# Moving the eight late adaLN modulation blocks of a hybrid backbone step from the recurrence stage to the projection stage, with a newly searched instruction order

## The chip, the core and the metric

The kernel runs on one core of a Trainium2 chip. The metric is the device time of one execution in microseconds, median of the runs; before the change three runs gave 1770.6 us (1767.48 to 1778.25). In what follows PE is TensorE, DVE is VectorE, ACT is ScalarE, POOL is GpSimd and SP is SyncE, which here only issues DMAs.

## The reference

One layer of a diffusion backbone is applied to 1024 latent tokens and 128 context tokens of 1024 features. Everything is f32.

```python
mod  = silu(c) @ ada_w + ada_b                 # (1024) @ (1024, 6144), for c and for c_ctx
shift1, scale1, gate1, shift2, scale2, gate2 = split(mod, 6)
h = rmsnorm(x, norm_mix_w) * (1 + scale1) + shift1
u = h @ w_in                                   # 1024 -> 4320 features
o_a = hgrn2_mixer(u[:, :2560])                 # 4 heads x 128, gated linear recurrence, both directions
o_b = rwkv7_mixer(u[:, 2560:])                 # 8 heads x 64, delta-rule state, both directions
x = x + gate1 * (concat(o_a, o_b) @ w_out)
h = rmsnorm(x, norm_ffn_w) * (1 + scale2) + shift2
x = x + gate2 * ((gelu(conv(h @ w_gate) + b) * (h @ w_up)) @ w_down)
y = rmsnorm(x, final_norm_w)
```

`shift1` and `scale1` (the first 2048 of the 6144 columns of `mod`) are needed by the first projection. The other 4096 columns, `gate1`, `shift2`, `scale2` and `gate2`, are needed only after the mixers.

## The kernel before

The kernel is written as a list of recorded operations, and a table puts them in order. `plan` records each call of an engine; a run of matmuls written under `plan.together()` is one operation and stays in one piece. `SEQUENCE` gives the order of all operations in the program, `ENGINE_OF` says for operations that may run on one of several engines (copies on ACT or DVE, stores issued by POOL or SP) which one it is, and `PLACE_OF` says for each tile which of its tag's buffers it takes. All three tables are numbers found by a search outside the kernel. An engine executes its own operations strictly in the order of `SEQUENCE`; semaphores make it wait for what it reads and for buffers to come free. All loads go through SP in that same order.

The work falls into five stretches on PE:

1. The start: the tokens are normed and transposed, and `mod_columns` computes the first 2048 columns of the modulation.
2. The projections: `proj` (L1070 to L1072) multiplies 128 columns of `w_in` with all 1152 tokens as three matmuls of 384 columns for each of 8 pieces of the contraction (two fp32r halves of weight and activation, three products). Between them stand the features of the RWKV mixer (`features`) and `elim`, which inverts the 32x32 blocks of the chunk systems. `elim` runs four times for the four head pairs `p` and once for the context; its PE work is L1462 and L1464, in PSUM tiles of the tag `el`.
3. The chains: `chains(g)` for the two groups `g` steps 18 times through the chunks of the RWKV recurrence. A step is `load_step` and `load_values` (L1694, L1696, L1703), the score products (L1713), a transpose (L1727), then L1760, a copy (L1762), L1767, a copy (L1769), L1775 and the outputs L1784 and L1786. `hgrn_block` (L1567 to L1633) and `hgrn_out` (L1658 to L1673), the last quarter of the projections (576 of the 2304 matmuls) and the first output projections (`wo_tile`, L1955 to L1957) are mixed in.
4. The output projection, norm and modulation of the remaining tiles.
5. The FFN: gate and up (L2065), then down (L2229).

`ada_block(b)`, b = 0 to 7, computes 512 of the late 4096 columns of `mod`. The bias `ada_b` is loaded as 4 rows (L966) into the tile `adab`, and 4 matmuls with the small constant `one` (L970) put it into one PSUM tile of the tag `a`. Four loads (L973) bring 512 KB of `ada_w` each into `adaw2`, which has two buffers, one in the SBUF tile `top` and one in `fx`; after each load 8 matmuls of 128 columns (L977), four at a time on different 32-column groups of PE, are added to the same PSUM tile. So one PSUM tile is held from the bias to the last of the 36 matmuls. ACT copies it to `adam` (L978), POOL or SP stores what is needed as rows (L980, L983), PE transposes it (L985) and DVE copies two columns of 4 into `modc` (L988). The tag `a` has four PSUM banks, which the chains and `hgrn_block` use as well. The loop over the chains calls `ada_block` after every second chunk step, so all eight blocks lie in stretch 3.

Names such as `top`, `low` and `fx` are large SBUF tiles in which `Layout` and `plan.tag` place the small ones; in the profile's rows and in the order an operand carries the name of the large tile. `banks` is all of PSUM.

Of the kernel before, what the change touches and what calls it, by code (L numbers as in the profile page):

```python
# [20 lines left out]
P = 128  # L21
# [3 lines left out]
KT = 8  # L25
NPAIR = 4
# [2373 lines left out]
```

## Time and profile before

| | |
|---|---|
| median of 3 runs | 1770.6 us |
| the profiled execution | 1778.03 us, span 1776.3 us |
| mean granted TensorE clock | 0.991 |
| PE busy | 1711.1 us, 96% of the span |
| DVE, ACT, POOL busy | 1424.9, 949.4, 354.6 us |
| moved by DMA | 352.97 MB, mean 199 GB/s |

The profile describes one execution, whose own time lies 7.4 us above the median of the runs. Its page gives the busy time of each engine, the span in 40 slices, the chain of work that ended last and the costliest groups of instructions. The trace behind it answers three more kinds of question that are used below: the busy time of each engine in a stretch of the span, who waited for whom in such a stretch, and the instructions in order of time. In an answer in order of time the second column is how long an instruction (or several alike) took by the record, and in brackets stands how long the engine sat idle before it and for whom. Matmuls overlap, so that the price of a group of matmuls is read from the start of the group to the start of the next instruction, not from the second column. A matmul in plain f32 has two records, one in fp32r has one.

### The profile page before, as it was taken

What the parts mean: (1) busy time and instruction counts of PE and PEld (TensorE: products, weight loads), DVE (VectorE), ACT (ScalarE), POOL (GpSimd) and SP (SyncE); (2) the same over time, 40 slices, a digit from 0 to 9 for tenths busy, and PEclk for the clock granted to TensorE, in tenths of its full rate; (3) what the DMA queues carried; (4) which work ended last, traced back from release to release, by engine and by line L of the source; (5) the groups of instructions that cost most, each with busy time, mean ns of one, the idle gap of its engine ahead of it and who ended that gap; (6) DMA issues with size and microseconds to landing.
All of it is one profiled execution on the core that took longest, in us unless ns stands there. A gap on an engine that the chain in (4) does not pass through costs nothing.

```text
span 1776.3 us, 44618 instructions
## 1 busy us (share of the span) xinstructions
PE 1711.1 (96%) x17726; PEld 1544.9 (87%) x17726; DVE 1424.9 (80%) x2722; ACT 949.4 (53%) x1977; POOL 354.6 (20%) x546
## 2 busy tenths in 40 slices
PE   6999999999999989999999999999999999999998
PEld 4888888889988888887877889999999999888886
DVE  6548988988787878786767888898888888979765
ACT  6655766662266655564645664444444444665542
POOL 2003133153311011112210013323333322000000
PEclk8999999999999999999989999999999999999999
DMA  9326456486676678889987657877877777898683
GB/s 308 98 86 163 109 136 154 120 227 208 183 225 196 203 214 277 275 279 265 312 245 271 224 120 146 176 152 160 170 156 153 158 158 157 274 316 275 196 273 130
DMA packets 341838, 352.97 MB, mean 199 GB/s; under 512 B 69817, under 2 KB 264398, under 8 KB 341278
## 3 DMA queue, kind: packets, MB, share of 16 engines
q1 hardware_dynamic: 287518, 284.85, 52.9%
q0 software_dynamic: 54112, 65.27, 19.2%
q8 instruction: 139, 2.28, 0.5%
q14 instruction: 69, 0.57, 0.1%
HBM read 254.99 MB, written 118.10 MB: 210 GB/s over the span
## 4 chain that ended last, share of the span: by engine, by line
PE 73%; DVE 4%; DMA 4%; ACT 3%; issue 1%; POOL 1%; SPq 0%; DVEq 0%; ACTq 0%; POOLq 0%
PE banks L2065 27%; PE banks L2229 14%; PE banks L1070 4%; PE banks L1072 4%; PE banks L1071 4%; PE banks L1713 2%; PE banks L1955 1%; PE banks L1957 1%; PE banks L1956 1%; PE banks L1582 1%; PE banks L1784 1%; PE banks L1627 1%; PE banks L1760 1%; PE banks L1767 1%; PE banks L1786 1%
## 5 line engine op out<-in xcount | busy, mean ns | idle before, releaser
L1070 PE MATMUL banks<-hh,wh 128*128 128x384 f32 x768 | 278.2, 362 | 0.6 <-DVE fx L1250 0.6
L1072 PE MATMUL banks<-hh,wl 128*128 128x384 f32 x768 | 258.7, 337 | 0.0
L1071 PE MATMUL banks<-hl,wh 128*128 128x384 f32 x768 | 258.4, 336 | 0.0
L2153 DVE SCALAR_TENSOR_TENSOR low<-low,pf 128x1024 f32<-128x1024 f32 x176 | 225.7, 1282 | 10.6 <-ACT low L2147 8.0
L2065 PE MATMUL banks<-qm,wh 128*128 128x320 f32 x968 | 223.4, 310 | 0.2 <-ACT wh L2035 0.2
L2065 PE MATMUL banks<-hbm,wh 128*128 128x256 f32 x880 | 162.9, 282 | 1.5 <-ACT low L1935 1.5
L2065 PE MATMUL banks<-qm,wl 128*128 128x320 f32 x528 | 162.8, 308 | 0.2 <-DVE wl L2035 0.2
L2065 PEld LDWEIGHTS banks<-qm,wh 128*128 128x128 f32 x968 | 161.0, 189 | 0.6 <-ACT wh L2035 0.5
L1070 PEld LDWEIGHTS banks<-hh,wh 128*128 128x128 f32 x768 | 144.8, 188 | 15.7 <-issue 9.3
L1071 PEld LDWEIGHTS banks<-hl,wh 128*128 128x128 f32 x768 | 145.2, 189 | 2.7 <-issue 1.2
L1072 PEld LDWEIGHTS banks<-hh,wl 128*128 128x128 f32 x768 | 144.9, 189 | 0.0
L2065 PEld LDWEIGHTS banks<-hbm,wh 128*128 128x128 f32 x880 | 139.3, 190 | 1.8 <-ACT low L1935 1.7
L2065 PE MATMUL banks<-ham,wh 128*128 128x256 f32 (+1 forms) x616 | 131.7, 294 | 0.0
L2065 PE MATMUL banks<-hbm,wl 128*128 128x256 f32 x440 | 124.4, 283 | 0.0
L2102 ACT COPY fx<-banks 128x256 f32<-128x256 f32 (+1 forms) x132 | 52.0, 397 | 110.2 <-PE banks L2065 98.2
L2065 PEld LDWEIGHTS banks<-ham,wh 128*128 128x128 f32 x616 | 101.4, 190 | 0.3
L2065 PEld LDWEIGHTS banks<-qm,wl 128*128 128x128 f32 x528 | 99.1, 188 | 0.4 <-DVE wl L2035 0.4
L2035 ACT CAST wh<-low 128x512 fp32r<-128x512 f32 x82 | 50.5, 618 | 69.4 <-PE banks L2065 60.5
L2065 PEld LDWEIGHTS banks<-hbm,wl 128*128 128x128 f32 x440 | 84.0, 191 | 0.0
L2065 PE MATMUL banks<-ham,wl 128*128 128x256 f32 (+1 forms) x264 | 77.0, 292 | 0.0
L2035 DVE TENSOR_TENSOR wl<-low,wh 128x512 fp32r<-128x512 f32 x82 | 56.2, 689 | 22.8 <-ACT wh L2035 20.7
L2035 ACT CAST wh<-wr 128x512 fp32r<-128x512 f32 x72 | 44.6, 622 | 54.3 <-PE banks L2065 43.8
(586 smaller groups left out, 4368.2 us busy)
## 6 DMA issues: line engine op xcount, KB each, us to landing
wr<-in_w_in_dram SPq DMA_DIRECT2D x34, 512.0 KB
d_t<-in_ffn_w_down_dram POOLq DMA_DIRECT2D x60, 256.0 KB, 6.5
low<-d_a SPq DMA_DIRECT2D x54, 256.0 KB
low<-d_ak SPq DMA_DIRECT2D x64, 192.0 KB
low<-d_kb SPq DMA_DIRECT2D x36, 256.0 KB
d_a<-low POOLq DMA_DIRECT2D x16, 576.0 KB, 4.7
top<-in_ada_w_dram SPq DMA_DIRECT2D x17, 512.0 KB
low<-in_ada_w_dram SPq DMA_DIRECT2D x32, 256.0 KB
```

Source lines behind the costliest of these rows:

```text
L1070: mm(o, wh[:, kt, :], hh[:, kt, c], kt == 0, False)
L1071: mm(o, wh[:, kt, :], hl[:, kt, c], False, False)
L1072: mm(o, wl[:, kt, :], hh[:, kt, c], False, kt == KT - 1)
L1582: mm(pv[r, i, :], xs[:, t0:t0 + 32], view(qy, t0, [[2 * m, 16 // m], [B + m, 2], [1, m]]), True, True)
L1627: mm(ps[:, i * P:(i + 1) * P], kt[:, i * P:(i + 1) * P], val[:, i, :], True, True)
L1713: mm(pa[h][:, P * w:P * w + P], kb[hc[h], w, :], W[hc[h], A0[h] + 192 * w:A0[h] + 192 * w + P], True, True)
L1760: mm(R[hc[h], 64 * w:64 * w + 64], av(h, w, 0), X[h][:, 0, w], True, True)
L2035: split(*w, src)
L2065: pe.matmul(o, a[:, kt, :], b[:, kt, :], start=start and first, stop=last, skip_group_check=not start)
L2102: act.copy(keep[n], y[:, 0:w])
L2153: dve.scalar_tensor_tensor(av, shifted(dy, dx), tap(3 * dy + dx), av, MUL, ADD)
L2229: pe.matmul(o, x, y, start=fresh and f, stop=l, skip_group_check=not fresh)
```

## The change

`ada_block` is called twice after each of the four `elim` calls of stretch 2, and no longer in the loop over the chains. Its bias rows now go into the zeroed tile `adam` itself, and the constant `one` has 128 rows. The sum over the four loads is no longer kept in PSUM: each group of 8 matmuls has a PSUM tile of its own (tag `el`, half a bank, now freed as soon as it is read); the first is copied to `adam` by ACT and the other three are added to it by DVE. `adaw2` and `adam` get places of their own in the first layout of `top`, one buffer each, for which the tile `ttd` of `elim` moves into `asys` and `pm` into `etmp`. All three tables are new; the words that came with the change say that the search's model now has the fetching of instructions in blocks. Matmuls are as many as before on PE (12977 instructions both times), DVE gets 24 additions, POOL 8 memsets.

```diff
-    N0, N1, NX = 9584, 14336, 4096
+    N0, N1, NX = 9584, 14368, 4096
...
-        .add("ako", 1024).add("asys", 1024).add("tsys", 1024).add("etmp", 256).add("ttd", 1024) \
-        .add("tn", 1024)
+        .add("ako", 1024).add("asys", 1024).add("tsys", 1024).add("etmp", 256) \
+        .add("tn", 1024).add("adaw2", 1024).add("adam", 128)
...
-        .add("lnr", 1024).add("sm", 32, 2).add("adab", 128).add("adam", 128)
+        .add("lnr", 1024).add("sm", 32, 2)
...
-    plan.tag("adaw2", [(top, 8786), (fx, 1536)], 1024)
...
-    plan.tag("el", [(mp, 512 * 6 + 256 * b) for b in range(4)], 256)
+    plan.tag("el", [(mp, 512 * 6 + 256 * b) for b in range(4)], 256, True)
...
-    one = cst("one", [4, 4, 32])
-    dve.tensor_copy(one, view(ident[0:4, :], 0, [[1, 4], [0, 32]]))
+    one = cst("one", [P, 4, 32])
+    dve.tensor_copy(one, view(ident, 0, [[1, 4], [0, 32]]))
...
     def ada_block(b):
 
         c0 = 2048 + 512 * b
-        br = tl("adab", [4, P])
-        ld(br, I["ada_b"][0, c0:c0 + 512].rearrange("(a b) -> a b", b=P))
-        ps, mr = pbank("a"), tl("adam", [P, P])
-        with plan.together(mr):
-            for q in range(4):
-                mm(ps[32 * q:32 * q + 32, 0:P], one[:, q, :], br, True, False)
+        mr = tl("adam", [P, P])
+        pool.memset(mr, 0.0)
+        ld(mr[0:4, :], I["ada_b"][0, c0:c0 + 512].rearrange("(a b) -> a b", b=P))
         for k0 in range(0, KT, 2):
+            ps = pbank("el", 256)
             w = tl("adaw2", [P, 2, 512])
             ld(w, I["ada_w"][0, k0 * P:(k0 + 2) * P, c0:c0 + 512].rearrange("(a p) n -> p a n", p=P))
             with plan.together():
+                if k0 == 0:
+                    for q in range(4):
+                        mm(ps[32 * q:32 * q + 32, 0:P], one[:, q, :], mr, True, False)
                 for a in range(2):
                     for q in range(4):
-                        mm(ps[32 * q:32 * q + 32, 0:P], sT[:, k0 + a, :], w[:, a, P * q:P * q + P], False, k0 + a == KT - 1)
-        act.copy(mr, ps[:, 0:P])
+                        mm(ps[32 * q:32 * q + 32, 0:P], sT[:, k0 + a, :], w[:, a, P * q:P * q + P], k0 > 0 and a == 0, a == 1)
+            if k0 == 0:
+                act.copy(mr, ps[:, 0:P])
+            else:
+                dve.tensor_tensor(mr, mr, ps[:, 0:P], ADD)
...
-        pq = pbank("a")
+        pq = pbank("el", 256)
...
-        ttd, tn = tl("ttd", [P, 32, 32]), tl("tn", [P, 32, 32])
+        ttd, tn = tl("asys", [P, 32, 32]), tl("tn", [P, 32, 32])
...
-        pm = tl("asys", [P, 8, 32])
+        pm = tl("etmp", [P, 8, 32])
...
         elim(*sys_, 32, p, "el")
+        for b in range(2):
+            ada_block(2 * p + b)
...
-    ctx_ = tl("ttd", [P, NPAIR, 128])
+    ctx_ = tl("tn", [P, NPAIR, 128])
...
-        if n % 2 == 0 and n:
-            if n // 2 <= 8:
-                ada_block(n // 2 - 1)
```

Three places show how the new order differs. The changed kernel's line numbers are 3 to 6 higher: its L978 is the L977 of before, its L1074 to L1076 are the projections L1070 to L1072, and so on as named.

The first place is on PE at the beginning of the projections, where the LoRA gate's small product (L1305 before, L1309 now) stands between projections. Before:

```order
L1070 MATMUL banks<-hh,wh_134 128x384
L1071 MATMUL banks<-hl,wh_134 128x384
L1072 MATMUL banks<-hh,wl_135 128x384
L1305 MATMUL banks<-low 128x512 x2
L1070 MATMUL banks<-hh,wh_134 128x384
L1071 MATMUL banks<-hl,wh_134 128x384
```

And now, with the second group of 8 modulation matmuls (L978) among them:

```order
L1074 MATMUL banks<-hh,wh_134 128x384
L1075 MATMUL banks<-hl,wh_134 128x384
L1076 MATMUL banks<-hh,wl_136 128x384
L1309 MATMUL banks<-low 128x512 x2
L978 MATMUL banks<-top,sT 32x128 x8
L1309 MATMUL banks<-low 128x512
L1074 MATMUL banks<-hh,wh_134 128x384
```

All 32 groups of 8 have moved into this stretch in this manner, each by itself; 24 projection matmuls and three L1309 lie between this group and the next one.

The second place is on PE late in the chains, at one of the last steps. Before, the modulation matmuls of block 7 (L970, L977) stand between a chain's L1760 and its L1767, and behind that:

```order
L1713 MATMUL banks<-low 128x128 x8
L1760 MATMUL banks<-low 64x64 x8
L970 MATMUL banks<-top,one 32x128 x4
L977 MATMUL banks<-top,sT 32x128 x8
L1767 MATMUL banks<-low 64x64 x8
L977 MATMUL banks<-fx,sT 32x128 x8
L1760 MATMUL banks<-low 64x64 x8
L1775 MATMUL banks<-low 64x64 x8
```

Now, at about the same step (L1766 was L1760, L1719 was L1713, L1773 was L1767, and L1958 to L1960 is the output projection):

```order
L1766 MATMUL banks<-low 64x64 x8
L1719 MATMUL banks<-low 128x128 x8
L1773 MATMUL banks<-low 64x64 x8
L1958 MATMUL banks<-ham,wh_134 128x512
L1959 MATMUL banks<-ham,wh_134 128x512
L1960 MATMUL banks<-ham,wl_136 128x512
L1766 MATMUL banks<-low 64x64 x8
```

Between a chain's two products now stands the other chain's score product, and an output projection where the second modulation group was.

The third place is SP's queue. Before, late in the chains, it ran as follows (L1696 loads the chain's matrices, L973 is the modulation's load, L966 its bias):

```order
L966 DMA top<-in_ada_b_dram 4x128
L973 DMA top<-in_ada_w_dram 128x2x512
L1696 DMA low<-d_ak_80 64x768
L1861 DMA top<-d_vb 128x1024
L983 DMA d_g_68<-top 2x128
L1703 DMA low<-d_v_85 64x4x64
L1696 DMA low<-d_ak_80 64x768
```

These loads now stand early in the projections (L971 was L973, L967 was L966, L1272 loads a projection's weights):

```order
L1272 DMA wr<-in_w_in_dram 128x8x128
L967 DMA top<-in_ada_b_dram 4x128
L1311 DMA d_g<-low 128x512
L971 DMA top<-in_ada_w_dram 128x2x512
L1272 DMA wr<-in_w_in_dram 128x8x128
L971 DMA top<-in_ada_w_dram 128x2x512
L1363 DMA d_v_84<-top 128x3x128 x2
```

Of the 32 loads of the modulation blocks 30 now stand in SP's queue ahead of the first load of the chains, and the last two just behind it; on PE all 32 groups stand ahead of the first score product of the chains.

More of the change, by code (lines that the diff above doesn't have):

```diff
@@ L122 @@
 SEQUENCE = [int(i) for i in """
[301 rows of a table removed]
[302 rows of a table added]
 """.split()]
 ENGINE_OF = (
-    "VVVAVAVAAAAAAVAVVVAVAAAVGGGGGSGGGGGSSGSSGGGAVAVVVAAVVVVAVVAVAAAAVVAVVVAAVVVVVAVAGASASASASASASVSASVVAGAASVAVASGSSAAAASSGSAAASAASAAAASSSSVAVASGSSAAVSSGV"
-    "SGVAAAAVAGSSGSGGSAAVAVAAGSSSSGGGSSSAGAGAGAAAAVVAAGSSSSGSSGGGGSSGSSGSGGGGGAAASGVSAAAVSSGSVAAVGSGSAVAGGASAAVASSSGAVAASSSSAAVSSAASSVAAAVAVSGGSSSGSAAAAAAA"
-    "SSGSSGSSGSSAGAGASAAAAVAAAGSSSGGGSGSSSSSSGSSGSSGSSAAAGGVGAVAASSGGVAVASGGSAAASAASAAAVSGGSVAAASGSSVAVGSGAGSVAVAAAASSSSSSGSAAVAAAASGSSSSGSSGSSSSAAAAVAAASG"
-    "GGSGGGSGGGSSGGGSGSGSSGAAASAAGVVAASSSSVAAAGSSSVAASAASVAAASSSSVAAASGSSVAASGAAGSVVAAAAVGSGSGGGSVAVAAAAGGGGSSSSGGGVAAAAAAAGGGGSSGSGGGSGGGGSGGSGSSGAASAASAA"
-    "SAGASASASASAGGSGAASAVSVASAGAGASAGASASGSGAASAASAASVSASASVSVSASSSGAASAASAASGSGSSSSGSGSGVVAAAVVGSSGGGGSGSGGGSGGSGSSGGSGAAAAAAAAVAAVVAAAGGAAAAAAGAAASGAAAA"
-    "GAASAGAAAAGGASASSAAAAAVAAAAAAAAASSAAVASSAAAAAAAAAAAAGGAASSVAAAVAAAAAAAAAASSVAAASSAAAAAAAGAGAAAAAGAGASSAAAAAAAAAAAAAAASSAAAASSSSSSGAAAVGAAVAAAAGAAASGAA"
-    "AAAAAAAAAAAAASGAAAASSAAVAAAASAGAAVAGAASAGAAAAAAAAVAAAAAASGAVVASGAAAVGAAAAAAAGAAAGSAAAAAAAAAAAAVAASSAAAASSSGSSSAAAAAGASAGAAAVGGAGASAAAAAVAAAAAVAAASSAAV"
-    "ASGAVAAGGAAAAAAAGAASGVAAVAAAAAAAAAAASSAAAASSAAAVGGAGASAAAAGGASAGAAAAAAAAAVAAAAASSAAVASSSSSGSAAAAAGGAAAAAAVAGAAGSVAAAAAAAAAAAAAASSAAVASSAAVAGGAAGAGAGAG"
-    "GGGAAAAAAAGAVGVGASGSSAAAAAAVAAAAAAAASGAAVASSAAAVAAAAAVVAGAAASSAAAAAAAAAAAAAAASSAAAVGSGSGGGAAAAGGASASAAVVGGVSAGSSGSAAAAGGAAAAAVGGAASGAAAAAGASASAAAAGGAS"
-    "ASGGSGAAAAGGVAAAAVGGVASSVVAVASAGVAVAASAGAAAASSSSSSSSSSSSSSSVAAAAAVASAAVAVAVAGGGGSGGSSGGGSGGSSGGGGGGGGGGGGGGGGGGGGGGGGGGGGGSGGGGSSSSSSSSSSSSSSSSSSSSSSS")
@@ new lines @@
+    "VVVAVAVAAVAAAAAAVVAVVAAASSSSSSSSGGGGGSGGGSSVVAVAVVAAVVAAVVAAVAAVVAAVAAAAVAVAVVVASAGASAGASVSAGAGASVVVSGASVVVASSSSAVAASSGSVAASAASAAAVGGSSVAAVGSGGAAAGGGV"
+    "SGVVAAAVASSGSSGSSAVVAVAAGSSGSSGGGSSASASAGAAVAAVAASSGSGGGGSSGSSSGSSGSGSSSGGSAAASGAGVAAASSGGVAAVGSSGVAASGASVAAASGSGAAVASSSSVAVSGAASGVVVAVAAGSSSSGSSVVAAA"
+    "AASGGSSSSSSGSAGAGASAAAAAAAASGGSGGSSSSGSSSSSSSGSSGGSAAASAASAAVASSSGVVVASSGSVAASAAGVVAVSSGGVAAASSSSVAAGSAVSSAAVVVVASGGGSGSSAAAAAAASSSSSSGSGSSSSGAAAAAAAA"
+    "GGSSGGGGSGGGGSSGSSGSGSGSAAASGAGVAAASSSGAAAASSGGVAASAASVAAASSSSVAAASSSGVAAGSGASSVVVAAAASSSSGGGGVVAAAAAGGGSSGGGSGSAVAAAAAAGGGGGGSGSGSGGGSGGSSSGGSSGGGGGS"
@@ new lines @@
+    "GSAASAASVASVSVGASASASAGSSGAAGAVGAASASAGAGASASASGSGAVSAASVAGVGASASVSAGASGGGAASAAGAASSSSGSGSGSGGGVVAAAVAGSGGGGSSGGSSGGGGGGGGSSSSAAAVAAAAVAVAAAAVAGAAVAAA"
+    "AGAAGSAAAAGGASASAAVAGAVSASAAAAAAAAAAAAAAASSAAVASSAAAAAGAAAAAAGAVAGGAAAAVAAAAAAAAAASSAAAAGSAAAAGAVSASAAAAAGAGAGAAAAAAAVAAAAVAASSAAAASSSSSGSAAVAGGAAAAAV"
+    "GAAAGGAAAAAAAAAAAAAAASSAAAAGGAAAVAAAGASAAAVAGAGAGAAAAAAAAAAAAAAASSAAVAGSAAAAAAAAAAAAGGAAGSAAAAAAAAAAAAAAVSGAAAAGSGGSGGAVAAGGAGAGAVAAGAAGAGAAAAAAAAAAAA"
+    "AAASSAAAASGAAAAGGAAAAAAGGAASSVVAVAAAAAAAAAAVSSAAAASGAAAAAAAGASAAAAAGAGASAAAAAAAVAAAAAAASSAAVASSGGSSGAAAAAGGAAAAAAAAGAASGAAAAAAAAAAAAAAAGSAAAAGGAAVAGGA"
@@ new lines @@
+    "AAAGAGAGGSSAAAAGGGGAVGVGASSSSAVAAAAAAAAAVAAASGAVVASSAAAVAGAVAAAVGGAASSAAAAAAAAAAAAAAASGAAAASSGGGGSAAAAGGAGAGAAVVGGVGAGAAAAGGAAAAAAAGAAGSAAAAGAAGASAAAA"
+    "GAAGASAAAAGGAAAAAAAAAVSGVVAAASVSVAVAASASAAAASGSGSSSSSSSSSSSVAAAAAVVGAAVAVAVAGGSSSSGGSGSSSSGGSSSGGGGGGGGGGGGGGGGGSSSGSGGGGGSSGGGSSSGSGSSSSSSSSSSGGSSSSS")
+PLACE_OF = (
+    "301286021164205633477410031320132320102031030123423013111000102013012340100210523140211047614023411105074210303013243101001010101001110110010131101001"
+    "100000100111010010010111100100111000001111000010110011100001120010111101100001101110110201313223131311010101101111010110010110100110101001101101001010"
+    "111101100110100101000100111100001110011100000202011121002110101110111111010010110010110000001011101001011011000110001011110003001011110110001011101033"
+    "321021111333121110111000101100110001000011111000111001001001011111101001100000111102200022023120000011101001101110101010000010100110111000101010001000"
+    "101011001110101011100010110011111100111000000010010110011110011110001010001111100010110000011010110000111000011100001011001111101000100000001100100020"
+    "121301010121023100101013212111002030002313101101032100100002112101130032210030000211101332323213313312021100001001101120001113010003212111030201101101"
+    "010201101002211121021321330100011201100020001321110000301001101112310020010011010011311001103130102003010110121110231231010101000310311102322321121300"
+    "110102100023021001310010313001011310000101010102003000121011000310001311310002000101101121013131024270301a103559167d329f463b88e1ac2b0edcf1330201110021"
+    "110113110002000141200011310014121100011013310010300103101100012013010010001103101100210000103021019082314567a01210102310210013201323011232001002110310"
+    "103230120198364571010230102030010022311121130211020122301120203022110030020032310120001101103220011232200231031112122020010023212300131121320130032001"
+    "111301210001311222033111030010121002310103221122131001220133010122021301022210110332210021132102022113310211000201211202100133331102002101120202120330"
+    "111201030210122003301211100221201002330131111021102001120203300112223301130221101001110102323022020031100130231120123101022311011022023101133112101010"
+    "201022311000311123100130211121013110212300202101031021132322111001001123100200101202230133102131001010200213102231131021131002112012301013120211130020"
+    "020133132001121310102023100021233111032022131020201013321110210110020133301010122110121000201312023101030232120003110102321001021210020013201682015473"
+    "1400213o2i3k020l1m1p2m383w0c160a2j33290o1s1l3e2n0h0u1v29382b34021c103s2y4m5i2l0d1b3o2w051q3k2g0f1x340t2013390j2z1c3e0i1h2u101035432023013p07521r66413x"
+    "2a5w1n4v214232100561j1ms3t8b5230g0qi2uy3614251co0pdl3054736f2k2r1625x1140a0h3406e3wn19jv2516m2zu2sip430553t10qo62160k2ga17em4536n3fs1cuc2100g0xq248z21"
+    "401u0w3t2z0539112k371a0n335130542f3s1q042g3x0d1w302t0j213401233y1942251i315o0u3a274f282k3n041b6e0v132h2r0s143221403412")
```

17 lines of the change are left out of this document (removed), and 603 rows, old and new, of the table SEQUENCE.

## The prediction

> **What bounds the kernel now.** I read the page first: its totals and the rows of 40 slices.
>
> ```profile
> span 1776.3 us, 44618 instructions
> PE 1711.1 (96%) x17726; PEld 1544.9 (87%) x17726; DVE 1424.9 (80%) x2722; ACT 949.4 (53%) x1977; POOL 354.6 (20%) x546
> PE   6999999999999989999999999999999999999998
> DMA  9326456486676678889987657877877777898683
> ```
>
> PE is busy for 1711.1 of 1776.3 us. Whatever changes the time must either change PE's work or fill part of the remaining 65.2 us, so the next question is where they lie. The busy time by stage answers it. Its columns are stretch, length, busy time of PE, PEld, DVE, ACT and POOL, granted TensorE clock, DMA share and GB/s; the stretches are the start, the projections, the chains, the rest of the output projection, FFN up and FFN down.
>
> ```profile
> 0.00:50.00 50.00, 36.38 (x275) 25.43 (x275) 32.85 (x97) 35.45 (x73) 9.52 (x29) 0.90 0.94 303
> 50.00:484.00 434.00, 428.30 (x4440) 386.63 (x4434) 338.92 (x685) 246.12 (x494) 112.97 (x215) 1.00 0.55 148
> 484.00:950.00 466.00, 431.57 (x7824) 377.33 (x7822) 361.14 (x868) 262.04 (x613) 79.70 (x146) 0.98 0.82 248
> 950.00:1037.00 87.00, 84.34 (x466) 70.34 (x460) 72.78 (x135) 59.19 (x129) 5.72 (x5) 1.00 0.71 230
> 1037.00:1520.00 483.00, 482.70 (x3627) 482.63 (x3628) 421.06 (x614) 220.57 (x430) 143.47 (x148) 1.00 0.76 156
> 1520.00:1776.30 256.30, 247.76 (x1112) 202.59 (x1110) 198.12 (x326) 126.07 (x242) 3.25 (x4) 0.99 0.75 245
> 650.00:900.00 250.00, 233.42 (x4315) 205.61 (x4304) 195.76 (x476) 143.34 (x328) 45.83 (x83) 0.99 0.91 278
> ```
>
> PE idles 13.6 us in the start, 5.7 in the projections (1.3%), 34.4 in the chains (7.4%), 2.7 behind them, 0.3 in FFN up and 8.5 in FFN down, almost all of that at the very end. The FFN is full and keeps its matmuls, so its 739 us stay, and the change can act only up to 1037 us. The chains are the loose stretch, and also the one in which DMA is busiest: 0.82 of the engines' time, 0.91 between 650 and 900 us, against 0.55 in the projections. The change takes work and loads out of the loose stretch and puts them into the full one. For the chains I asked for what PE waited there (who waited, for what: us in total, times, longest).
>
> ```profile
> PE banks L1713 <- DMA low<-d_ak: 5.8, 4, 2.5
> PE banks L1767 <- ACT low L1762: 3.2, 3, 1.6
> PE banks L977 <- DMA fx<-in_ada_w_dram: 1.1, 2, 0.7
> PE banks L977 <- DMA top<-in_ada_w_dram: 1.1, 1, 1.1
> PE banks L1727 <- DMA low<-d_kb: 1.0, 1, 1.0
> PE banks L1713 <- DMA low<-d_akp: 0.7, 1, 0.7
> ```
>
> Loads account for 9.7 us, of which 2.2 are the modulation's own; the other 24.7 of the 34.4 us are short waits for ACT and DVE, of which the second row is the longest kind.
>
> **Part 1: PE work added to the projections.** Nothing of a modulation block leaves PE; 32 groups of 8 matmuls, 8 biases and 8 transposes change their place. What a group of 8 costs by itself is seen where one stands before a projection (start, duration, instruction; 16 records are 8 matmuls).
>
> ```profile
> 742.08 0.33 PE L1071 MATMUL banks<-hl,wh 128*128 128x384 f32 x1
> 742.25 0.34 PE L1072 MATMUL banks<-hh,wl 128*128 128x384 f32 x1
> 742.52 0.40 PE L1582 MATMUL banks<-top 128*32 128x32 f32 x24
> 742.73 0.62 PE L977 MATMUL banks<-top,sT 128*32 128x128 f32 x16
> 743.28 0.44 PE L1070 MATMUL banks<-hh,wh 128*128 128x384 f32 x1
> 743.56 0.34 PE L1071 MATMUL banks<-hl,wh 128*128 128x384 f32 x1
> 693.90 0.42 PE L970 MATMUL banks<-top,one 4*32 4x128 f32 x8
> 694.25 0.40 PE L1582 MATMUL banks<-top 128*32 128x32 f32 x24
> 745.41 0.27 PE L985 MATMUL banks<-c_ident,top 128*128 128x128 f32 x1
> 745.61 0.40 PE L1582 MATMUL banks<-top 128*32 128x32 f32 x24
> ```
>
> From 742.73 to 743.28 the group costs 0.55 us. The projection behind it takes 0.28 instead of the 0.17 between two projections, and the projection ahead of the small matmuls 0.27: another 0.10 on each side. A group alone between projections thus costs 0.75, one beside other small work 0.55. By the new order 15 of the places have projections on both sides, 15 on one side and 10 on none, so I take 0.65: 32 x 0.65 = 20.8. The biases take 0.35 (693.90 to 694.25), 8 of them 2.8; the transposes 0.20 (745.41 to 745.61), 8 of them 1.6. Together **+25.2 us**, between 22.0 (all at 0.55) and 28.4 (all at 0.75). The projections are 98.7% full on PE, so nothing hides it.
>
> The Trainium skill (TensorEngine Tiling (Array Packing), Key Properties) says that changing the tiling mode drains TensorE, which speaks against setting 32-column groups singly between full-width projections. By that rule alone the dearer end would hold for every group, 28.4 instead of 25.2. The trace agrees that there is such a price, with 0.10 us on each side.
>
> DVE gets 24 additions of 128x128 out of PSUM. Their form is not in the trace. The nearest rows are the smaller copy of 128x4 (L988) and the addition of 128x256 (L1793), median ns in the middle:
>
> ```profile
> L988 DVE COPY modc<-banks x16: 143/152/163, 668.4 to 937.4; 128x4 f32<-128x4 f32 x16
> L1793 DVE TENSOR_TENSOR low<-banks,low x16: 405/420/425, 514.6 to 934.2; 128x256 f32<-128x256 f32 x16
> ```
>
> Between 0.15 and 0.42, halfway 0.29, is 7 us in all; DVE has 434 - 338.9 = 95 us free there, and no projection waits for a sum. I take 0 on the path; without the cover it would be 7. The 8 memsets are POOL's, which is idle for three quarters of this stretch: also 0.
>
> **Part 2: PE work gone from the chains.** The instructions of the two lines, taken alone in the same stretch (L970, then L977):
>
> ```profile
> 484.00:950.00 466.00, 3.60 (x64) 1.27 (x64) 0.98 0.82 248
> 484.00:950.00 466.00, 19.57 (x512) 12.98 (x512) 0.98 0.82 248
> ```
>
> With 1.6 for the transposes this is 24.8 us of busy time, but it overlaps with its neighbours. From start to start, a group of 8 costs 0.55 alone and less when two follow each other, as they do in most places here: with 0.40 for those it would be 32 x 0.40 + 2.8 + 1.6 = 17.2 (0.40 is my estimate from the 0.55 above less most of the switching). I take the middle, 21, so **-21 us**, between -17.2 and -24.8. Parts 1 and 2 together are **+4.2 us**, from -2.8 to +11.2: cutting the sum into four separate groups makes PE's work a little dearer.
>
> **Part 3: loads.** 31 or 32 loads of 512 KB, 16 MB, leave a stretch that moves 248 GB/s x 466 us = 116 MB: 14% less. What this can give is read from a step near the end of the chains. First PE, with the wait in brackets, then what SP issued ahead of it:
>
> ```profile
> 908.94 1.28 PE L1713 MATMUL banks<-low 64*128 64x128 f32 x16 [2.48 <-DMA low<-d_ak]
> 910.15 1.12 PE L1760 MATMUL banks<-low 128*64 128x64 f32 x16
> 911.20 0.65 PE L970 MATMUL banks<-top,one 4*32 4x128 f32 x8
> 911.78 1.08 PE L977 MATMUL banks<-top,sT 128*32 128x128 f32 x16
> 912.79 1.12 PE L1767 MATMUL banks<-low 128*64 128x64 f32 x16
> ```
> ```profile
> 896.58 0.38 SPq L973 DMA_DIRECT2D top<-in_ada_w_dram  x1
> 898.04 0.45 SPq L1696 DMA_DIRECT2D low<-d_ak  x1
> 902.73 0.46 SPq L1696 DMA_DIRECT2D low<-d_ak  x1
> ```
>
> The chain's second matrix load was issued at 902.73 behind a modulation load of twice its size, and PE stood for 2.48 us at 908.94. With the loads gone the modulation's own 2.2 us go for certain, and of the other 7.5 I take 40%, 3: **-5.2 us**, between -2.2 and -9.7. What is late next in such a step is the copy of L1762, part 4.
>
> In the projections the same loads meet DMA engines at 0.55; 16 MB at the 303 GB/s that the start reached are 53 us of the 434, so they fit. SP's queue is what they can hold up: `adaw2` has one buffer, so a load can be issued only when the group before it is done, and the projection weights and the features' stores behind it wait as well. On average the groups are 434 / 32 = 13.6 us apart; I take 0 and price the case as a rival.
>
> **Part 4: cover.** The rows above show what the modulation did beside its own work: it stood between L1760 (910.15) and L1767 (912.79), which needs ACT's copy of L1760's result. Elsewhere L1767 waited 3.2 us for that copy. In the new order the other chain's score product fills this place, but something has to; the blocks appeared at 33 places of PE's order in the chains. If one place in eight opens by 0.5 us, a third of the longest such wait of 1.6, this is **+2 us**; bounds 0 and 33 x 0.5 = +16.
>
> **Part 5: the new order as such.** It was searched anew for the whole program. Of the 24.7 us that PE waits for ACT and DVE in the chains, the best case is the projections' rate of 1.3% of 466, 6 us, which would be -18.7; nothing in the trace excludes the same on the other side. The freed PSUM banks point to a gain: a block held one of the four `a` banks from its bias to its last matmul, for instance b = 7 from 911.20 on, and the chains and `hgrn_block` wait for the same four. I take a quarter of the best case, **-5 us**, between -18.7 and +18.7.
>
> **The sum** is +25.2 - 21 - 5.2 + 2 - 5 = -4.0 us. Against the profiled execution's own 1778.0 (span 1776.3) this is 1774.0; that execution lies 7.4 above the median of the runs, 1770.6, so I predict 1766.6 for the median.
>
> **Rivals.** *The chains close up.* If loads were what kept them loose and the new order uses the freed banks, their idle time falls from 34.4 to the projections' 6: -28.4, with the +4.2 of PE work -24.2, so 1746. For it speak the DMA share of 0.91 and that the chain of waits between 880 and 930 us runs mostly over loads; against it, that only 9.7 us of PE's waits are for loads.
>
> *The modulation was the filler, and the chains do not shrink.* The place is the chain step L1760, L1762, L1767, L1769, L1775: if the two chains' own waits set the length of the stretch, taking 21 us of filling work out of it only turns them into idle time, while the projections get their +25.2. With the 2.2 us of the modulation's own waits gone this gives +23, so 1794. It decides for slower by over 1% from the point where the idle time of the chains passes 34.4 + 17.7 - 4.2 = 48 us. For it speaks that 24.7 of the 34.4 us are waits for ACT and DVE; against it, that PE is 93% busy there, and that other work (576 projection matmuls, the output projection) is still there to fill with.
>
> *The loads come late in the projections.* Between the second and third group lie 24 projections at 0.17 and three other matmuls, some 5 us, and a late load of the modulation took, in the chain of waits:
>
> ```profile
> 924.44 5.70 DMA fx<-in_ada_w_dram
> ```
>
> If a third of the 24 loads inside blocks came 1.5 us late, PE would lose 12 us: 1779, within 1%. Against it: DMA was at 0.80 where that load ran.
>
> **How the numbers follow.** About 1% (17.7 us) is what a measurement of this kernel can tell from no change. My forecast, a small gain that stays within 1%, has 0.56; the chains closing up 0.26; the filler 0.12; late loads 0.06. Faster by over 1% (below 1752.9) comes from the second, 0.26; slower (above 1788.3) from the third, 0.12; the rest, 0.62, is the same. The forecast's own terms reach from about 1748 to 1784. The range takes in the closing up, 1746, with some room for part 3, and stops short of the filler's 1794: 1740 to 1788.
>
> **What would show it.** In the profile after: no modulation matmul behind the first score product; the first L1713 some 20 to 28 us later than at 484 (part 1); from there to the first FFN matmul some 24 to 34 us less than 553 (parts 2 to 5); DMA share in the chains near 0.7; waits of L1713 for d_ak below 4 us; FFN unchanged at 739 us. The prediction is wrong if PE's idle time in the chains moves by more than 17 us either way, or if PE waits for `ada_w` in the projections by more than a few us.

## The result, and the profile after

The changed kernel takes 1801.26 us (median of 6 runs, 1796.81 to 1803.74) against 1772.65 us for the kernel before beside it: ratio **1.016**, 95% interval 1.0138 to 1.0183, so 24 to 32 us slower. The forecast was 1766.6, the range ended at 1788. The profiled execution took 1803.7 (span 1802.0), near the upper end of its runs.

The totals and slices of the page after:

```profile
span 1802.0 us, 44632 instructions
PE 1722.8 (96%) x17726; PEld 1544.0 (86%) x17726; DVE 1434.9 (80%) x2748; ACT 940.4 (52%) x1971; POOL 360.2 (20%) x570
PE   6998899999999999998999999999999999999998
DMA  9435475668767666886987667777877777798774
```

PE is busy for 11.7 us more than before (1711.1) and idle for 14 us more. For a fair comparison by stage the marks must be events, not times: the first score product of the chains (L1713 before, L1719 after), the first FFN matmul, the end. Windows of before, then of after, with the columns of the prediction's table:

```profile
50.00:483.80 433.80, 428.10 (x4439) 386.43 (x4431) 338.92 (x685) 245.92 (x494) 112.90 (x214) 1.00 0.55 148
483.80:1024.40 540.60, 506.17 (x8224) 439.25 (x8221) 423.19 (x982) 313.14 (x724) 82.90 (x149) 0.98 0.81 247
1024.40:1776.30 751.90, 740.40 (x4802) 693.84 (x4801) 629.92 (x959) 354.92 (x687) 149.30 (x154) 1.00 0.75 186
```
```profile
50.00:529.50 479.50, 460.05 (x5041) 405.08 (x5039) 354.85 (x750) 240.43 (x493) 119.67 (x232) 0.99 0.61 170
529.50:1043.30 513.80, 486.57 (x7637) 421.83 (x7637) 418.95 (x958) 311.58 (x723) 88.55 (x162) 0.99 0.74 227
1043.30:1802.00 758.70, 741.99 (x4802) 693.61 (x4800) 631.56 (x959) 354.98 (x687) 145.91 (x148) 1.00 0.75 185
```

The chains shrank as was forecast: 540.6 to 513.8, 26.8 us less, DMA share down from 0.81 to 0.74. The projections did not: 45.7 us more, of which PE is busy for 32.0 and idle for 13.7 (idle 5.7 before, 19.4 now). What PE waited for there, us in total, times, longest:

```profile
PE banks L1401 <- DVE top L1393: 3.5, 1, 3.5
PE banks L1347 <- DVE top L1343: 2.6, 1, 2.6
PE banks L978 <- DMA top<-in_ada_w_dram: 2.3, 1, 2.3
PE banks L1242 <- ACT fx L1238: 2.0, 2, 1.4
```

Only the third row is the modulation's. L1401 and L1347 are small matmuls of `features`, L1242 prepares the other mixer; all three stood in these same projections before, where the longest wait was 0.9. The longest of them on PE, with the projections ahead of it and behind it:

```profile
165.20 0.34 PE L1075 MATMUL banks<-hl,wh 128*128 128x384 f32 x1
165.38 0.34 PE L1076 MATMUL banks<-hh,wl 128*128 128x384 f32 x1
165.89 0.62 PE L978 MATMUL banks<-top,sT 128*32 128x128 f32 x16
170.02 0.21 PE L1401 MATMUL banks<-top 64*32 64x64 f32 x1 [3.51 <-DVE top L1393]
...
171.22 0.52 PE L1075 MATMUL banks<-hl,wh 128*128 128x384 f32 x1
171.54 0.52 PE L1076 MATMUL banks<-hh,wl 128*128 128x384 f32 x1
```

Behind the wait a projection starts every 0.32 us instead of every 0.17. The windows of 3.4 us before and after the wait show why (the column before the DMA share is the granted clock):

```profile
163.00:166.40 3.40, 3.40 (x40) 2.99 (x38) 2.42 (x4) 2.79 (x8) 1.05 (x3) 1.00 0.95 228
170.50:173.90 3.40, 3.40 (x25) 3.26 (x17) 3.34 (x8) 1.88 (x6) 1.39 (x3) 0.50 0.65 174
```

At half clock for 3.4 us, PE loses up to another 1.7 us, and this time counts as busy. Below, such a stretch is called a half-clock piece. The projections hold four of them after and one before, so up to 5 of the 32 us of busy time are lost to the clock, not to work.

### The profile page after: what moved, and what is told of

It is laid out like the page before. It is cut to its first block, busy times and chain, and to the rows that moved or that the text cites. A ratio compares the mean times of both kernels' runs of the same rounds, so it can differ in the third digit from the quotient of the medians.

```text
span 1802.0 us, 44632 instructions
## 1 busy us (share of the span) xinstructions
PE 1722.8 (96%) x17726; PEld 1544.0 (86%) x17726; DVE 1434.9 (80%) x2748; ACT 940.4 (52%) x1971; POOL 360.2 (20%) x570
## 4 chain that ended last, share of the span: by engine, by line
PE 37%; DMA 6%; issue 3%; DVE 2%; ACT 1%; POOL 1%; SPq 0%; DVEq 0%; POOLq 0%; ACTq 0%
PE banks L2068 21%; PE banks L2232 10%; PE banks L1958 1%; PE banks L1960 1%; PE banks L1959 1%; DMA wr<-in_ffn_w_down_dram 1%; DMA wr<-in_ffn_w_up_dram 1%; DMA low<-in_ffn_w_up_dram 1%; DVE low L2156 0%; DMA low<-in_ffn_w_down_dram 0%; DMA top<-in_x_sample_dram 0%; DMA d_t<-in_ffn_w_down_dram 0%; PE banks L1971 0%; DMA wr<-in_ffn_w_gate_dram 0%; DVE qm L2214 0%
## 5 line engine op out<-in xcount | busy, mean ns | idle before, releaser
L1074 PE MATMUL banks<-hh,wh 128*128 128x384 f32 x768 | 283.3, 369 | 0.6 <-ACT fx L1246 0.6
L1076 PE MATMUL banks<-hh,wl 128*128 128x384 f32 x768 | 260.2, 339 | 0.5 <-DVE wl L1272 0.5
L1074 PEld LDWEIGHTS banks<-hh,wh 128*128 128x128 f32 x768 | 146.0, 190 | 20.5 <-issue 11.8
L1076 PEld LDWEIGHTS banks<-hh,wl 128*128 128x128 f32 x768 | 145.5, 190 | 0.8 <-DVE wl L1272 0.8
L2105 ACT COPY fx<-banks 128x320 f32<-128x320 f32 (+1 forms) x132 | 51.9, 397 | 119.9 <-PE banks L2068 118.7
L2176 POOL DMA_DIRECT2D d_t<-in_ffn_w_down_dram x44 | 45.9, 1082 | 159.6 <-DMA d_t<-d_t 124.5
```

The source lines that it names most:

```text
L1074: mm(o, wh[:, kt, :], hh[:, kt, c], kt == 0, False)
L1076: mm(o, wl[:, kt, :], hh[:, kt, c], False, kt == KT - 1)
L2105: act.copy(keep[n], y[:, 0:w])
L2176: acc(td[j][k], b)
```

## Experiments

Ratios are to the kernel before on the same chip, with 95% intervals. "Proj." is 50 us to the first score product, "chains" from there to the first FFN matmul, both in us from each run's profile; "half clock" is the time at a granted clock of 0.50 in these two stretches. The runs were made on several chips, on which the kernel before took 1772.7 to 1775.4 us, so they are compared by ratio.

| run | median us | ratio | proj. | chains | half clock |
|---|---|---|---|---|---|
| before / after | 1772.7 / 1801.3 | 1.0160 (1.0138..1.0183) | 433.8 / 479.5 | 540.6 / 513.8 | 3.4 / 13.7, 17.1 / 6.8 |
| e1_free_loads | 1797.0 | 1.0137 (1.0120..1.0153) | 476.6 | 512.5 | 10.2, 0 |
| e2_no_loads | 1796.4 | 1.0133 (1.0118..1.0148) | 476.8 | 514.7 | 10.2, 0 |
| e3_one_matmul | 1797.6 | 1.0127 (1.0102..1.0153) | 474.5 | 517.3 | 20.5, 10.2 |
| a_move_old_order | 1834.2 | 1.0324 (1.0294..1.0354) | 502.4 | 529.1 | 41.0, 10.2 |
| b_new_order_no_move | 1864.3 | 1.0492 (1.0464..1.0521) | 459.4 | 599.3 | 17.1, 54.6 |
| f_old_ffn_order | 1797.6 | 1.0123 (1.0096..1.0149) | 479.3 | 518.2 | 10.2, 10.2 |
| c_thin_blocks_before | 1771.0 | 0.9981 (0.9963..0.9999) | 433.1 | 531.8 | 3.4, 10.2 |
| n_before_none | 1765.6 | 0.9948 (0.9928..0.9967) | 436.6 | 525.4 | 3.4, 10.2 |
| n_after_none | 1777.7 | 1.0018 (0.9996..1.0039) | 456.1 | 513.4 | 3.4, 3.4 |
| s_shared_buffers | 1773.9 | 0.9992 (0.9974..1.0011) | 433.2 | 533.9 | 3.4, 0 |
| p_old_proj_new_chains | 1761.7 | 0.9917 (0.9890..0.9943) | 438.1 | 521.4 | 3.4, 10.2 |

### Is it SP's queue and the loads?

SP's own waits in the projections of the changed kernel offered the first theory: it stands until PE has used the single buffer, and everything queued behind the load stands with it.

```profile
SPq L971 <- PE banks L978: 58.4, 17, 11.2
```

The first run frees the loads, the second takes their bytes away as well.

```diff
 e1 -  mm(ps[32*q:32*q+32, 0:P], sT[:, k0+a, :], w[:, a, P*q:P*q+P], ...)
    +  mm(ps[32*q:32*q+32, 0:P], sT[:, k0+a, :], ident, ...)
 e2    as e1, and
    -  ld(w, I["ada_w"][0, k0*P:(k0+2)*P, c0:c0+512]...)
    +  ld(w[:, 0, 0:1], I["ada_w"][0, k0*P:(k0+1)*P, c0:c0+1])
```

> The changed kernel with one edit: the modulation's matmuls read the identity instead of the loaded weights, so no load has to wait until PE has used the buffer; all loads, all PE work and the whole order stay (the modulation's values are left out by this). Theory Q (queue): SP stood 58.4 us in 17 waits for PE at the modulation load, stores of kb queued behind it landed late, DVE and then PE waited, and each long wait of PE was followed by 3.4 us at half clock; then PE's idle time in the projections falls from 19.4 by about 10 to 14 us, the half-clock pieces there from 4 to 1 or 2, and the time from 1801 to 1782..1788. Theory P (price on PE): the groups' own cost on PE is what was missed; then nothing changes, 1799..1803. Theory O (order): the waits belong to the new order of everything else; then 1799..1803 too, with the waits at L1401 and L1347 where they were.

> As the run before, and each modulation load also cut from 512 KB to 512 bytes: SP still issues it, nothing waits for it, and 16 MB of traffic are gone from the projections (the modulation's values are left out). Theory Q in its pure form (the queue position alone): the same time as with the free loads. Theory D (DMA traffic): the kb store that PE waited for at 170.0 us took 6.5 to 7 us to land while the DMA engines were full; then this run gains what the free loads did not, down to 1782..1788, while the free loads stay near 1800. Theories P and O: 1799..1803.

Theory Q forecast 1782 to 1788 and got 1797: the loads and their 58 us of SP waits are worth some 4 us (the 2.3 us wait of L978 with its half-clock piece), and even that lies within the intervals. Theory D fell too. P and O, with 1799 to 1803, are missed by 2 to 3 us, and this pair cannot tell them apart. The window of the projections in e1, and its longest waits, stand where they stood:

```profile
50.00:526.60 476.60, 459.75 (x5043) 404.14 (x5042) 354.39 (x751) 240.77 (x494) 119.01 (x232) 0.99 0.61 171
```
```profile
PE banks L1401 <- DVE top L1393: 3.0, 1, 3.0
PE banks L1347 <- DVE top L1343: 2.6, 1, 2.6
```

### Is it the blocks' work on PE?

```diff
 e3 -  the bias matmuls and 8 matmuls of 32 columns per group
    +  mm(ps[:, 0:P], ident, w[:, 1, 0:P], True, True)
 c  (in the kernel before)
    -  8 matmuls of 32 columns per group
    +  mm(ps[:, 0:P], ident, w[:, 1, 0:P], False, k0 == KT - 2)
```

> The changed kernel with each group of 8 (or 12) modulation matmuls replaced by one full-width 128x128 matmul that still reads the loaded weights (sums and biases are left out): loads, waits and order stay, PE loses 32 x 8 narrow matmuls and their tiling switches. Theory P: the projections lose 22 to 30 us of busy time, so 1801 falls to 1771..1779. Theories Q and O: only the bare 0.40 to 0.55 us of each group goes, about 13 to 17 us net of the one matmul that stays, 1784..1788, and PE's idle time in the projections stays at 19 us.

> The kernel before with each group of 8 modulation matmuls replaced by one full-width matmul (the modulation's values are wrong by this); loads, order and places stay. It asks what the blocks' PE work costs in the chains. If the chains are bound by PE, 10 to 14 us go: 1758..1763. If it was filler (the chains' own waits set the pace), it turns into idle time of PE: 1769..1774.

Both theories missed e3: PE's busy time in the projections fell by 10.5, as P says, but the time by only 5.0:

```profile
50.00:524.50 474.50, 449.55 (x4529) 402.73 (x4527) 354.50 (x750) 240.04 (x493) 121.01 (x232) 0.98 0.61 171
```

PE's idle time rose from 19.4 to 25.0 there, and the half-clock pieces from four to six. So in the new order these projections are no longer bound by PE alone: work taken off PE comes back as waits for ACT and DVE and as half-clock time. The same thinning in the chains of before took 3 us (0.9981), where chains bound by PE would have given 10 to 14. That is the filler's time, but not its mechanism: PE's idle time there is 33.1 us, against 34.4 in the quoted profile of before and 33.0 in s (below, same work and order), so it did not grow; instead the chains of c have 10.2 us at half clock where those of s have none.

The Trainium skill (TensorEngine Tiling (Array Packing), Key Properties) says that changing the tiling mode drains TensorE. e3 fits this but does not show it by itself, because the edit takes matmuls and changes of mode together: 256 matmuls fewer and no change of mode took 10.5 us of busy time off the projections, with two half-clock pieces more. In the chains, among tiles of 64 rows, the similar edit of c left 498.7 us of busy time against 506.2 and 500.9 in two profiles of the unthinned order, so at most 7.5.

### Is it the order? Hand-made mixtures

Run a gives the old order to everything but the blocks, which stay in the projections; run b gives the new order and puts the blocks back into the chains; f takes the old order for the FFN alone.

```diff
 a -  order, engines and places of after
   +  those of before; modulation behind the same counts of projections
 b -          for b in range(2): ada_block(2 * p + b)        # projections
   +          if n % 2 == 0 and n and n // 2 <= 8:           # chains
   +              ada_block(n // 2 - 1)
 f -  order, engines and places of after, from the first FFN-up weight on
   +  those of before
```

> The changed code (blocks in the projections, four parts of each sum, single buffers) with the order, engines and places of before for everything but the modulation; the modulation's operations stand behind the same numbers of projection matmuls as in the changed kernel. Theory M (the move): the blocks themselves cost the 45 us in the projections, wherever the rest stands: the time stays at 1793..1805. Theory O (order): the long waits of the changed kernel (L1401 3.5, L1347 2.6 us) and the 7 us in the FFN belong to the new order: they go, the projections grow by 25 to 32 us over before, the chains lose 17 to 25, the FFN returns to 752, and the time is 1772..1784. A loss in the chains beyond that would be the missing filler: 1790 or more with PE idle over 48 us there.

> The new order, engines and places for everything but the modulation, whose blocks are back in the chains, at the same counts of chain matmuls as before (with four parts of each sum, in the a banks). Theory M: the time returns to before's, 1770..1778, and the three long waits in the projections go. Theory O: the waits of L1401 and L1347 stay, the projections end 10 to 15 us later than before's 484 without a block in them, the FFN keeps its 7 us, and the time is 1788..1805 (the chains get the blocks back, some 20 us, at places that no search chose).

> The changed kernel with the order, engines and places of before from the first FFN-up weight on; all ahead of it as in the changed kernel. Theory O: FFN up and down take before's 752 instead of 758.7, so 1801 becomes 1793..1796. Theory M, or the FFN's 7 us being a matter of one profile: 1799..1803.

Run a met neither theory, run b went past both. The stages say why: the blocks, put by hand at places that no search chose, ruin the stage that they are in. In a, PE's longest waits in the projections are two of the blocks' own and one of `features`, and its half-clock pieces there come to 41 us:

```profile
PE banks L978 <- DMA top<-in_ada_w_dram: 7.9, 5, 2.4
PE banks L989 <- DVE top L982: 5.8, 1, 5.8
PE banks L1401 <- DVE top L1392: 4.1, 2, 3.8
```

In b it is the chains, at 599.3, with 54.6 us at half clock. So neither total says what the move costs. But one stage of b has no block in it and the new order throughout:

```profile
50.00:509.40 459.40, 440.95 (x4477) 393.52 (x4476) 349.77 (x713) 240.28 (x488) 116.39 (x221) 0.98 0.52 142
```

The projections take 459.4 us instead of 433.8 without any modulation. f won 0.37% by ratio, with intervals that overlap, so it decides nothing. Its FFN took 751.8 us. The changed kernel's profile shows 758.7 us from the first FFN matmul on, but e1, e2 and e3, in the same order, show 753: most of its 7 us belong to that one profile, 1 to 3 to the order.

### Two by two: order and blocks

To price both without places of my own, the runs n leave all blocks out of each kernel (`modc` is set to zero), keep each order as it stands, and run s asks apart what the shared buffers do.

```diff
 n -  ada_block(...)            # all eight, in before and in after
   +  pool.memset(modc[:, :, 16:48], 0.0)   # once, and 10 small stores
 s (in the kernel before, same order)
   -  ttd = tl("ttd"), pm = tl("asys"), ctx_ = tl("ttd")
   +  ttd = tl("asys"), pm = tl("etmp"), ctx_ = tl("tn")
```

> The kernel before without any modulation block (its values are set to zero once), all else in the same order. With the next run it makes a two-by-two: order by blocks. The thinned blocks took 3 us off the median; their loads go here too. If the blocks were filler, 1764..1770, with PE idle in the chains growing from 34 to 45 or more; if the chains were bound by PE and loads, 1745..1756.

> The changed kernel without any modulation block. Theory O (order): the projections stay 20 to 26 us longer than in the run before it (459 us with no block in them was seen when the blocks were moved back), with the waits of L1401 and L1347; the time is 1776..1784, slower than the kernel before though it has less to do. Theory M (the move): with the blocks go all 45 us of the projections; 1750..1760, as fast as or faster than the run before it.

> The kernel before with the three tiles moved to the buffers that the change uses (ttd in asys, pm in etmp, ctx_ in tn); same order on every engine. Theory O in its form 'the tables': no difference, 1770..1777. Theory B (buffers): the elimination now waits for the buffer before it is free, in both orders, and this is what slows the projections: 1782..1798, with new waits at L1401, L1462 or L1464.

The sharing does nothing. n_after_none came in at theory O's time, 1777.7, with waits at the same lines (its L1402 and L1348 are after's L1401 and L1347), though none of them is longer than 1.6 us. n_before_none came in at the filler's time, 1765.6, though PE's idle time in the chains rose to 38.7 only, not to 45. The blocks are worth 0.52% in the chains of the old order (1 less 0.9948) and 1.42% in the projections of the new one (1.0160 less 1.0018), 9.2 and 25.2 us of 1774. The new order costs 0.70%, 12.4 us, with no block in it. By the intervals each of the three is known to about 4 to 6 us. "The new order" is here all that the change brings beside the blocks: the three tables, the moved tiles (which s clears in the old order) and the earlier freeing of the tag `el`, which no run changed alone. First the old order, then the new, projections and chains:

```profile
50.00:486.60 436.60, 430.83 (x4456) 388.36 (x4454) 338.33 (x683) 245.69 (x494) 112.92 (x214) 1.00 0.55 148
486.60:1012.00 525.40, 486.74 (x7639) 424.32 (x7637) 420.55 (x966) 310.86 (x716) 80.60 (x145) 0.99 0.74 223
```
```profile
50.00:506.10 456.10, 436.00 (x4476) 389.09 (x4474) 349.49 (x715) 241.22 (x489) 115.26 (x220) 1.00 0.52 142
506.10:1019.50 513.40, 485.95 (x7638) 420.83 (x7638) 417.96 (x958) 312.04 (x723) 89.03 (x163) 1.00 0.74 228
```

In both traces exactly 4705 matmul records start before the first score product, so PE has the same to do: the new order takes 19.5 us more for it, 5.2 of busy time and 14.3 of waiting, and 12.0 us less for the chains (up to 3.4 of it for two half-clock pieces fewer). Both stretches of projections hold one half-clock piece, so there the clock is not the difference. What waits in the projections of the new order is no single thing (three of its rows):

```profile
PE banks L1348 <- DVE top L1344: 4.0, 3, 1.6
...
PE banks L1402 <- ACT low L1284: 1.6, 1, 1.6
PE banks L1402 <- ACT low L1418: 1.5, 1, 1.5
```

There are 14 waits of 0.6 us or more in these projections, against 3 in the old order. In the two traces the projections stand in 88 pieces between other PE work in the new order and 79 in the old, with a median of 9 records (1.8 us) against 12 (2.3 us). Shorter pieces cover less of what ACT and DVE do between two steps of the features. That this is the cause fits, but it is not shown, as no run changed it alone. A rival stands beside it: the new table of engines gives DVE more to do in the projections (busy 349.5 us against 338.3) and ACT less (241.2 against 245.7), and the waits for DVE grew from 3.0 to 8.0 us, those for ACT from 1.6 to 9.0.

### Can the good halves be joined?

```diff
 p (no blocks)
   -  the new order throughout
   +  the old order up to the first score product and from the first FFN-up weight on
```

> No modulation block; the order of before up to the first score product of the chains and again from the first FFN-up weight on, the new order between them. If the order's effect sits in its stages (projections 436.6 old against 456.1 new, chains to FFN 525.4 old against 513.3 new, FFN 751.6 against 754.4), the parts add up: 1765.6 - 12 = 1753..1756, faster than either kernel without blocks. If the new order buys its quicker chains with the slower projections (work done there that the chains then have not to do), the chains lose what the projections win: 1764..1778.

```profile
50.00:488.10 438.10, 431.56 (x4463) 388.86 (x4463) 339.15 (x685) 245.67 (x493) 108.81 (x211) 1.00 0.54 147
488.10:1009.50 521.40, 489.88 (x7639) 423.61 (x7637) 418.59 (x961) 310.64 (x722) 92.55 (x170) 0.99 0.74 225
```

Between the two answers: the projections are back at 438.1, but the chains keep only 4.0 of their 12.0 us, in a profile that lay 2.7 us above the median of its five runs and has two half-clock pieces more there than n_after_none. So about half to two thirds of what the new order wins in the chains hangs on what stands ahead of them. By the first score product the new order has 10 DVE instructions and 8 of SP's transfers more behind it, but 12 of ACT's fewer, so how much of this is work done ahead and how much has only changed its engine stays open. At 0.9917 this order is not told apart from n_before_none's 0.9948. With blocks at the price of 0.5% it would stand at about 0.997, which no measurement here would tell from the kernel before; no run has it.

## Why the prediction was wrong, point by point

- **Part 1, +25.2 (22.0 to 28.4): right in its mechanism; that the sum was met is partly luck.** By the stages of after and n_after_none the blocks add 23.4, by the ratios 25.2. A group alone between projections costs what was said, 0.58 us from 74.79 to 75.37 and 0.10 on each side:

```profile
74.52 0.34 PE L1076 MATMUL banks<-hh,wl 128*128 128x384 f32 x1
74.79 0.65 PE L978 MATMUL banks<-top,sT 128*32 128x128 f32 x16
75.37 0.44 PE L1074 MATMUL banks<-hh,wh 128*128 128x384 f32 x1
75.65 0.34 PE L1075 MATMUL banks<-hl,wh 128*128 128x384 f32 x1
```

  But PE's instructions are the same in after and n_after_none except for the blocks, so their steps, from start to start less the idle time, can be compared one by one. At full clock the blocks take 21 us (the groups 18.4, the biases 2.0, the transposes 0.7) and make their neighbours 1 us longer. That is 22 us, the forecast's lower end. About 4 us more are half-clock time: four pieces against one in n_after_none, a term that the forecast does not have. PE's idle time is no larger with the blocks than without (19.5 and 20.1), but its longest wait is 3.5 us instead of 1.8. The zeros for the sums, the memsets and the loads held to within e1's 4 us, and with them fell the rival of late loads, priced at 12.
- **Parts 2 to 4, -21 - 5.2 + 2 = -24.2: wrong, -9.2.** Part 2's price was right: from start to start the blocks' instructions take 21.8 us in the chains of the quoted profile of before and 20.7 in those of s, which has the same work in the same order:

```profile
483.20:1017.10 533.90, 500.94 (x8222) 434.51 (x8221) 422.82 (x982) 313.56 (x724) 83.28 (x149) 1.00 0.82 251
483.10:1014.90 531.80, 498.68 (x7776) 433.65 (x7773) 422.88 (x982) 312.53 (x724) 80.42 (x149) 0.99 0.82 251
```

  (The second row is c's.) But from s to n_before_none the chains are only 8.5 us shorter. Of the 20.7 us that left, 12.2 came back: 5.7 as idle time of PE (33.0 to 38.7), 4.1 in three half-clock pieces where s has none, and 2.4 as longer steps at full clock. The quoted profile of before had 17.1 us of half clock in its chains, which makes its 540.6 a high base. Part 4, the cover, had +2 for all of this. Without blocks PE waits 20.3 us for ACT in the chains instead of 13.7 and 10.4 for DVE instead of 8.9, +8 by these waits alone. And part 3's -5.2 is not confirmed: PE's waits for DMA in the chains were 9.7 in the quoted profile, but 3.7 in s with all loads in place and 3.6 in n_before_none without them, so most of that price was one execution's. The rows of n_before_none for the step named in the filler rival (L1769 is before's L1767, L1764 its L1762), and for d_ak (L1715 is before's L1713):

```profile
PE banks L1769 <- ACT low L1764: 4.6, 5, 2.0
PE banks L1762 <- ACT low L1771: 3.2, 2, 1.9
PE banks L1715 <- DMA low<-d_ak: 3.2, 2, 1.8
```

- **Part 5, -5: the step that failed most, +12.4.** I looked for the effect of the new order only where PE idled, in the chains, and there it was better than I took it, -12.0 by the stages without blocks, against +19.5 in the projections and +2.7 in the FFN. I left out the projections because PE was busy there for 98.7%, as if this were a property of the stage. It was one of the old order: a stretch that full had 5.7 us of idle time to win from a new order, and lost 19.5. Why the new order waits more there stays open, as said above.
- **The sum.** 25.2 - 9.2 + 12.4 = 28.4 us, which is the measured 1.6% (the three come from the same ratios, so they must add up, and that they do proves nothing). Against the forecast's terms, 15 us were missed in parts 2 to 4 and 17 in part 5.
- **The rivals.** The filler's 1794 lay nearest, but its mechanism is half of the story: the stretch did shrink (by 26.8 in the trace), because the new order closed it while the blocks left. The idle time that it made decisive, over 48 us in the chains, is 27.2; the loss sits in the projections. What it says of the chains is more than half right in the old order, where 12.2 of 20.7 us came back. The chains closing up to 6 us of idle time is refuted.
- **What was to be seen.** No L978 behind the first score product, a chain stretch 24 to 34 us shorter (26.8; the 553 that the forecast counted from ran to 1037 us, while the first FFN matmul stood at 1024.4, so the base is 540.6), DMA near 0.7 (0.74) and little waiting for d_ak came as said:

```profile
PE banks L1719 <- DMA low<-d_ak: 1.2, 2, 1.0
```

  The first L1719 came 45.7 us later instead of 20 to 28. "A few us" of waiting for the loads in the projections held (2.3). So neither of the two signs that were to show the prediction wrong appeared: the idle time of the chains moved by 7.2, not by 17. Both looked at the chains and the loads, and none at the waits of the projections for ACT and DVE, where it failed.

## What to carry to other kernels

When a change brings a newly searched order, price the order by itself and for every stage, the full ones first: where PE is 98.7% busy, the order has little to win and, here, lost 19.5 us. A block's price is that of its neighbours: the same eight blocks, some 21 us of PE work in both places, cost 9 us among the chains' short waits, 25 between full-width projections, and 66 (a: 502.4 less 436.6) to 86 (b: 599.3 less 513.4) at places put by hand. Leaving the moved work out of both versions gives a two-by-two that neither a hand-made undo nor thinning gave here. A wait of a few us needs a second profile of the same order before it is used as a price, and so does a stretch with half-clock pieces in it.

## What the hardware showed unexpectedly

A wait of PE can have an aftermath: in the changed kernel the granted clock stood at 0.50 for 3.4 us at the end of, or up to 1.0 us behind, waits of 3.5, 2.6, 2.3 and 1.4 us in the projections, up to 1.7 us lost each time, booked as busy. The Trainium skill (TensorE: Matmul & The Clock Gate, HAM oscillation — how this bites in real kernels) puts the limit at idle gaps of about 3.4 us; here gaps well below it were followed by the half clock, as behind the 2.62 us wait that ended at 217.25 us, though not every one: a wait of 1.6 us in the chains had none, nor had one of 3.1 us in b's. Nor does a piece need a long wait: the kernel before stood at half clock from 288.8 us on, where its longest wait since 200 us was 0.4. What decides it is not shown here. The 2.62 us wait and its piece:

```profile
217.25 0.80 PE L1347 MATMUL banks<-hsum,top 128*128 128x2 f32 x6 [2.62 <-DVE top L1343]
```
```profile
218.30:221.70 3.40, 3.40 (x13) 2.82 (x13) 3.30 (x6) 0.96 (x2) 1.26 (x2) 0.50 0.71 188
```
